# A fused streaming-encoder block: the weight sums of the short groups made in the output projection, part of the last operands split one block earlier

## The chip, the cores and the metric

The kernel runs on one core of a Trainium2 chip. The metric is the device time of one execution in microseconds (us). Three runs of the kernel before gave 2062.32, 2059.2 and 2062.35 us, a median of 2062.32 us.

In the text PE is the matrix engine, DVE the vector engine, ACT the scalar engine, POOL and SP the two engines that issue the DMA transfers. "hi" and "lo" are the two parts into which a 32-bit number is split for the matrix engine.

## The reference, cut to what matters

One layer works on 512 tokens of 2048 features: a mixer (convolution heads and gated linear attention), an output projection, and a feed-forward block of 8192 hidden features.

```python
y = concatenate([y_conv, y_gla], axis=-1)
x = x + y @ w_out                                   # output projection
h = rmsnorm(x, norm2_g)
x = x + square(relu(h @ w_ff1)) @ w_ff2             # feed-forward: FF1, FF2
return rmsnorm(x, norm_f_g)
```

All of it is in float32. The change touches how `w_ff2` is brought to the matrix engine for the last 1024 of the 8192 hidden features; what is computed stays the same.

## The kernel before, in words

**Products.** Every product of float32 operands is made of three passes on PE: hi times hi, hi times lo, lo times hi. For each tile of weights ACT makes hi (a cast) and DVE makes lo (raw minus hi). A product of two 2x2 arrangements of blocks is made in a scheme with seven products ("forms" 1 to 7) in place of eight. A form's weight operand is a quarter block (forms 1, 3, 2) or a sum of quarter blocks that DVE makes first (forms 5, 7, 6, 4), so DVE has four sums and seven lo tiles for each group of seven forms. `block_forms` (line 226) loads the four quarters on SP and makes sums and splits; `split_w` (line 212) is the split, whose ACT cast is on line 215 and DVE subtraction on line 216; `plus` is the sum on line 223.

**FF2.** The loop over `blk` (0 to 3) and `n` (0 to 3, the four quarters of the output features) runs two groups for each (blk, n). In blocks 0 to 2 a form has 24 matmuls in each group. In block 3 the first group is full and the second is *short*: half as many hidden features, so 12 matmuls for each form, while every form still needs its cast, its lo and, for four of them, its sum. In the second group `evict` (line 1014) takes the results out of PSUM: DVE makes t, x, v and four c tiles (line 1020), ACT scales each c in two pieces (line 1027), and POOL adds it to `c_keep` in DRAM with an accumulating DMA (line 1028).

**The last 512 hidden features** are not in any block. They come plain, in 16 groups `e_{i}{n}` of 12 matmuls (128x512 each) for four token tiles i and four output quarters n, in the order n = 0, 2, 1, 3. Their weight operands are w00, w01, w20, w21, w10, w11, w30, w31 (hi and lo of each), their activations e0 and e1. They are loaded and split after block 3's code: casts on line 1088, lo on line 1089. Each e group is added to x by DVE (line 1133), squared by ACT (line 1137) for the final norm.

**The output projection** comes earlier, in five chunks. In chunk 0 a unit has 24 matmuls of 128x512; DVE makes one lo for each unit and is idle for the rest of it. Its results are added to `xr`, the residual, whose 20 tiles POOL loads from `x`.

**What sets the order.** Each engine works through its own list in order. The lists are made by a scheduler, so that the place of an instruction there can differ from the code's. Raw weights come through one ring of four 512 KB slots (tag `raw`), hi and lo through rings of three, sums through a ring of two (tag `w`). A load is issued when the work that used its slot four loads before is done, and the loads stand in order on SP.

In names, `f_3114` is block 3, n = 1, group 1 (the short one), form 4, and `f_3201` is block 3, n = 2, group 0, form 1. `c_31` is a c tile of block 3, n = 1.

Of the kernel before, what the change touches and what calls it, by code (L numbers as in the profile page):

```python
# [8 lines left out]
F32 = mybir.dt.float32  # L9
# [5 lines left out]
P = 128  # L15
# [18 lines left out]
RAWS = 4  # L34
# [8 lines left out]
def hymba_kernel(  # L43
# [712 lines left out]
    for n, c in enumerate(chunks):  # L756
        for i in range(NT):
            nc.gpsimd.dma_start(xs[n][i], x[i * P : (i + 1) * P, c])
    ss2 = const_tile("ss2", [P, NT, 5])
# [53 lines left out]
    with tc.tile_pool(name="n2", bufs=1) as n2:  # L813
# [15 lines left out]

        for n in range(3):  # L830
            at = {2: (2 * n - 2,), 5: (2 * n - 1,)} if n else {}
            out_chunk(n, w_out, 8 * n, 8, 512, 2, pairs_at(at), w_ready if n == 0 else ())
# [166 lines left out]
    with tc.tile_pool(name="ff", bufs=1, reuse_waits="tile") as ff:  # L999
# [53 lines left out]

        for blk in range(4):
            for n in range(4):
                dst = {f: fbank(f"f2_{blk}{n}{f}") for f in ORDERS[1]}
                had = {}
                for grp in range(2):
                    m = 2 if (blk, grp) == (3, 1) else 4
                    src, i0 = (  # L1060
                        (w_ff2, 4 * (8 * blk + 2 * n + grp)) if blk < 3
                        else ((w_ff2, 4 * (24 + n)), (w_ff2_short, 4 * n))[grp]
                    )
                    forms = block_forms(src, i0, m * HALF, f"f2_{blk}{n}{grp}")
# [14 lines left out]
        slots = first + second[:7]  # L1079
        taken = [0]  # L1080

        def next_slot(name):
            taken[0] += 1
            return in_slot(slots[taken[0] - 1], name)

        def pair_split(src, name):
            hi, lo = next_slot(f"{name}h"), next_slot(f"{name}l")
            S.copy(hi, src)  # L1088
            V.tensor_tensor(out=lo, in0=src, in1=hi.bitcast(F32), op=ALU.subtract)
            return hi, lo  # L1090

        w2 = {}

        def last_weights(n):
            for j in range(2):
                raw = wp.tile([P, UNIT], F32, name=f"raw_e{n}{j}", tag="raw", bufs=RAWS)
                nc.sync.dma_start(raw[:, :1024], w_ff2_last[2 * n + j])
                hi, lo = pair_split(raw[:, :1024].rearrange("p (a b) -> p a b", a=4), f"w{n}{j}")
                for e in range(2):
                    w2[n, 2 * j + e] = [t[:, 2 * e : 2 * e + 2, :].rearrange("p a b -> p (a b)") for t in (hi, lo)]  # L1100

        load_x(3)
        order = (0, 2, 1, 3)
        last_weights(order[0])
# [19 lines left out]
        for i in range(NT):  # L1124
# [3 lines left out]
            for n in order:  # L1128
# [8 lines left out]
                S.activation(sq.rearrange("p a b -> p (a b)"), x3[n], AF.Square, accum_out=ss3[:, i, n : n + 1])  # L1137
# [18 lines left out]
def laid_out(inputs):  # L1156
# [29 lines left out]

    def feature_pairs(w):
# [25 lines left out]
        "w_ff2_short": quarters(ff2[7168:7680], 2).reshape(-1, P, 512),  # L1213
# [21 lines left out]
```

## Time and profile before

| | |
|---|---|
| median of three runs | 2062.32 us (2059.2 to 2062.35) |
| profiled execution, its own time | 2064.88 us |
| its span | 2063.2 us, so 1.68 us lie around it |
| PE busy | 2026.6 us, 98% of the span |
| DVE busy | 1594.4 us, 77% |
| ACT busy | 1018.4 us, 49% |
| POOL busy | 224.1 us, 11% |
| mean granted clock of PE | 0.996 |

A row of a timeline gives the start, the time taken, the engine, the line, the operation, its output and inputs, the shape and, in brackets, how long the engine was idle before it and what ended that. Matmuls overlap: the distance between two starts tells more than the time of one. A row of the view of waits gives total time, number of times and the longest.

### The profile page before, as it was taken

The page shows a single profiled execution, that of the slowest core. Times are in us where ns is not written, and L with a number is a line of the kernel's source. Part 1 is how long each engine was busy: PE and PEld are TensorE (multiplying, and loading weights), DVE is VectorE, ACT ScalarE, POOL GpSimd, SP SyncE. Part 2 cuts the span into 40 slices and gives each one's busy share as a digit, 9 for nine tenths or more (in the row PEclk, how much of TensorE's full clock was granted, in tenths as well). Part 3 has the DMA queues.
Part 4 walks back from the last instruction along what each step waited for, and adds up shares of the span by engine and source line. Part 5 has one row for each costly group of instructions (what it writes and reads, how often), then busy time and mean ns, then how long its engine had stood idle before and what let it go on. Part 6 is the DMA issues. An engine that isn't in the chain of part 4 may idle for free. (4 is left out here: it accounts for less than half of the span.)

```text
span 2063.2 us, 36979 instructions
## 1 busy us (share of the span) xinstructions
PE 2026.6 (98%) x15344; PEld 1945.0 (94%) x15344; DVE 1594.4 (77%) x1880; ACT 1018.4 (49%) x1366; POOL 224.1 (11%) x349
## 2 busy tenths in 40 slices
PE   8999999999999989999999999999999999999997
PEld 8999998888888889999999999999999999999995
DVE  8778775677734478888888888888789779788785
ACT  8434444433433345555555545555455445545453
POOL 1000001100020001000101001111011111111321
PEclk9999999999999999999999999999999999999999
DMA  8333335322253325545545545758477567657764
GB/s 283 128 124 133 132 135 180 123 87 72 82 197 111 110 82 176 174 147 183 168 147 177 164 163 165 220 178 274 126 226 217 148 193 232 150 164 236 169 186 119
DMA packets 112554, 334.57 MB, mean 162 GB/s; under 512 B 12213, under 2 KB 29157, under 8 KB 112384
## 3 DMA queue, kind: packets, MB, share of 16 engines
q1 hardware_dynamic: 60912, 210.92, 30.9%
q0 software_dynamic: 51472, 121.27, 21.2%
q8 instruction: 120, 1.97, 0.4%
q14 instruction: 50, 0.41, 0.1%
HBM read 263.20 MB, written 68.94 MB: 161 GB/s over the span
## 5 line engine op out<-in xcount | busy, mean ns | idle before, releaser
L1009 PE MATMUL f<-lo_f,ah 128*128 128x256 f32 x1568 | 442.3, 282 | 1.7 <-DVE lo_f L216 1.5
L1009 PE MATMUL f<-hi_f,ah 128*128 128x256 f32 x1568 | 440.3, 281 | 1.0 <-ACT hi_f L215 1.0
L1009 PE MATMUL f<-hi_f,al 128*128 128x256 f32 x1568 | 440.6, 281 | 0.0
L215 ACT CAST hi_f<-w_f 128x1024 fp32r<-128x1024 f32 (+1 forms) x256 | 261.5, 1023 | 337.4 <-PE f L1009 114.3
L216 DVE TENSOR_TENSOR lo_f<-w_f,hi_f 128x1024 fp32r<-128x1024 f32 (+1 forms) x256 | 304.8, 1191 | 150.0 <-ACT hi_f L215 148.9
L1009 PEld LDWEIGHTS f<-lo_f,ah 128*128 128x128 f32 x1568 | 295.5, 188 | 2.9 <-DVE lo_f L216 2.7
L1009 PEld LDWEIGHTS f<-hi_f,ah 128*128 128x128 f32 x1568 | 296.2, 189 | 1.4 <-ACT hi_f L215 1.4
L1009 PEld LDWEIGHTS f<-hi_f,al 128*128 128x128 f32 x1568 | 296.2, 189 | 0.0
L215 ACT CAST hi_f<-raw_f 128x1024 fp32r<-128x1024 f32 (+1 forms) x192 | 196.5, 1024 | 141.9 <-PE f1b L933 54.5
L216 DVE TENSOR_TENSOR lo_f<-raw_f,hi_f 128x1024 fp32r<-128x1024 f32 (+1 forms) x192 | 227.4, 1186 | 20.8 <-ACT hi_f L215 20.8
L223 DVE TENSOR_TENSOR w_f<-raw_f,raw_f 128x1024 f32<-128x1024 f32 (+1 forms) x128 | 152.4, 1190 | 14.4 <-DMA raw_f<-in_w_ff 9.1
L223 DVE TENSOR_TENSOR w_f<-w_f,raw_f 128x1024 f32<-128x1024 f32 (+1 forms) x128 | 152.3, 1190 | 3.6 <-DMA raw_f<-in_w_ff 0.3
L933 PE MATMUL f1c<-Sh,hi_f 128*128 128x256 f32 x512 | 144.5, 282 | 0.9 <-ACT q L957 0.9
L933 PE MATMUL f1a<-Sh,hi_f 128*128 128x256 f32 x512 | 145.3, 284 | 0.0
L933 PE MATMUL f1a<-Sh,lo_f 128*128 128x256 f32 x512 | 145.2, 284 | 0.0
L933 PE MATMUL f1a<-Sl,hi_f 128*128 128x256 f32 x512 | 145.1, 283 | 0.0
L933 PE MATMUL f1c<-Sh,lo_f 128*128 128x256 f32 x512 | 144.5, 282 | 0.2 <-DVE lo_f L216 0.2
L933 PE MATMUL f1c<-Sl,hi_f 128*128 128x256 f32 x512 | 144.3, 282 | 0.0
L78 PE MATMUL tm_op<-hi_op,yh 128*128 128x512 f32 (+1 forms) x304 | 106.3, 350 | 0.0
L79 PE MATMUL tm_op<-lo_op,yh 128*128 128x512 f32 (+1 forms) x304 | 105.4, 347 | 0.0
L80 PE MATMUL tm_op<-hi_op,yl 128*128 128x512 f32 (+1 forms) x304 | 105.1, 346 | 0.0
L1028 POOL DMA_DIRECT2D c_keep<-c x64 | 56.4, 900 | 385.9 <-ACT c L1027 292.6
(521 smaller groups left out, 5564.7 us busy)
## 6 DMA issues: line engine op xcount, KB each, us to landing
raw_f<-in_w_ff SPq DMA_DIRECT2D x240, 512.0 KB, 3.4
st<-a_keep POOLq DMA_DIRECT2D x33, 512.0 KB, 5.2
c_keep<-c POOLq DMA_DIRECT2D x64, 256.0 KB, 4.9
a_keep<-y POOLq DMA_DIRECT2D x14, 896.0 KB, 4.8
raw_op<-in_w_out SPq DMA_DIRECT2D x22, 512.0 KB, 3.3
raw_v<-in_w_v SPq DMA_DIRECT2D x16, 512.0 KB, 3.5
raw_og<-in_w_pairs SPq DMA_DIRECT2D x16, 512.0 KB, 3.3
raw_cc<-in_w_feat SPq DMA_DIRECT2D x16, 512.0 KB, 3.7
```

Source lines behind the costliest of these rows:

```text
L78: T.matmul(dst, l[0], r[0], start=start, stop=False)
L79: T.matmul(dst, l[0], r[1], start=False, stop=False)
L80: T.matmul(dst, l[1], r[0], start=False, stop=stop)
L215: S.copy(hi[:, :n], src)
L216: V.tensor_tensor(out=lo[:, :n], in0=src, in1=hi[:, :n].bitcast(F32), op=ALU.subtract)
L223: V.tensor_tensor(out=w, in0=in0, in1=in1, op=ALU.add)
L933: T.matmul(dst[:, :HALF], l[:, c], r, start=start and p == m == 0, stop=p == 7 and m == 2, skip_group_check=True,)
L1009: T.matmul(d, l[:, k, t], r[:, c], start=grp == k == i == e == 0, stop=grp == 1 and k == m - 1 and e == 2, skip_group_check=True,)
L1028: nc.gpsimd.dma_start(c_keep[n][q], t, accum_op=ALU.add)
```

## The change

Three things are done.

1. **The sums of the four short groups** (16 DVE additions of 128x512) are made during chunk 0 of the output projection, after its units 1, 3, 5 and 7. `sum_short(n)` loads the four quarters in two loads of 512 KB through the raw ring, makes the four sums in two tiles of the `w` ring, and POOL stores these two tiles (512 KB each) in DRAM scratch `short_sums`. In block 3 a short group then loads two tiles of quarters and two of ready sums (`short_forms`: three loads of 512 KB and one of 256 KB, where before there were four of 256 KB) and makes no sum. The host lays `w_ff2_short` out anew so that forms 1 and 3 lie in one tile.
2. **Part of the last operands is split earlier**: e0 and e1 in the first group of (3, 1), w00 in the first group of (3, 2). They and w01 go to tiles of the `stage` pool and a new ring `early`. The activations e0 and e1 come through the raw ring.
3. **ACT's squares** of token tile 0 are ordered behind the last weight cast (`issue_after`), and `gft` is loaded later.

```diff
@@ -756,6 +758,25 @@
+
+    short_sums = [[tc.dram_tile([P, 1024], F32, name=f"short{n}{m}") for m in range(2)] for n in range(4)]
+
+    def sum_short(n):
+        raws = []
+        for m in range(2):
+            raw = wp.tile([P, UNIT], F32, name=f"raw_s{n}{m}", tag="raw", bufs=RAWS)
+            nc.sync.dma_start(raw[:, :1024], w_ff2_short[2 * n + m])
+            raws.append((raw[:, :512], raw[:, 512:1024]))
+        (b12, b21), (b11, b22) = raws
+        w56, w47 = (sums[-1].tile([P, 1024], F32, name=f"w_s{n}{m}", tag="w", bufs=2) for m in range(2))
+        for out_, i0, i1 in (
+            (w56[:, :512], b11, b12), (w56[:, 512:], w56[:, :512], b21),
+            (w47[:, :512], w56[:, 512:], b22), (w47[:, 512:], b11, b21),
+        ):
+            V.tensor_tensor(out=out_, in0=i0, in1=i1, op=ALU.add)
+        for m, w in enumerate((w56, w47)):
+            nc.gpsimd.dma_start(short_sums[n][m], w)
+
...
@@ -827,9 +848,13 @@
+        def shorts(j):
+            if j % 2:
+                sum_short(j // 2)
+
         for n in range(3):
             at = {2: (2 * n - 2,), 5: (2 * n - 1,)} if n else {}
-            out_chunk(n, w_out, 8 * n, 8, 512, 2, pairs_at(at), w_ready if n == 0 else ())
+            out_chunk(n, w_out, 8 * n, 8, 512, 2, pairs_at(at) if n else shorts, w_ready if n == 0 else ())
...
@@ -1051,22 +1076,77 @@
 
+        def short_forms(n):
+            v = {}
+            for m, (src, c, fs) in enumerate((
+                (w_ff2_short[2 * n], 0, (1, 3)), (short_sums[n][0], 0, (5, 6)),
+                (short_sums[n][1], 0, (4, 7)), (w_ff2_short[2 * n + 1], 512, (2,)),
+            )):
+                raw = wp.tile([P, UNIT], F32, name=f"raw_f{n}{m}", tag="raw", bufs=RAWS)
+                nc.sync.dma_start(raw[:, c:1024], src[:, c:])
+                for i, f in enumerate(fs):
+                    v[f] = raw[:, c + 512 * i : c + 512 * (i + 1)]
+            return lambda f: split_w(v[f], 512, f"f2_3{n}1{f}")
+
+
+        early = [(stage, "st", 4)] * 4 + [(ff, "early", 2)] * 2
+        slots = [slot + (1,) for slot in first + second[:7]]
+        taken = [0]
+
+        def next_slot(name):
+            if early:
+                pool, tag, bufs = early.pop(0)
+            else:
+                pool, tag, bufs = slots[taken[0]]
+                taken[0] += 1
+            return pool.tile([P, 4, HALF], F32R, name=name, tag=tag, bufs=bufs)
+
+        def pair_split(src, name):
+            hi, lo = next_slot(f"{name}h"), next_slot(f"{name}l")
+            last_cast[0] = S.copy(hi, src)
+            V.tensor_tensor(out=lo, in0=src, in1=hi.bitcast(F32), op=ALU.subtract)
+            return hi, lo
+
+        w2 = {}
+
+        def last_weights(n, j):
+            raw = wp.tile([P, UNIT], F32, name=f"raw_e{n}{j}", tag="raw", bufs=RAWS)
+            nc.sync.dma_start(raw[:, :1024], w_ff2_last[2 * n + j])
+            hi, lo = pair_split(raw[:, :1024].rearrange("p (a b) -> p a b", a=4), f"w{n}{j}")
+            for e in range(2):
+                w2[n, 2 * j + e] = [t[:, 2 * e : 2 * e + 2, :].rearrange("p a b -> p (a b)") for t in (hi, lo)]
+
+        order = (0, 2, 1, 3)
+        a = []
+
+        def last_acts(g):
+            raw = wp.tile([P, UNIT], F32, name=f"raw_a{g}", tag="raw", bufs=RAWS)[:, :1024]
+            raw = raw.rearrange("p (a b) -> p a b", a=4)
+            nc.sync.dma_start(raw, a_last[g])
+            hl = pair_split(raw, f"e{g}")
+            for e in range(2):
+                a.append([[t[:, (1, 0, 2, 3)[2 * e + row], :] for t in hl] for row in range(2)])
+
+
+        early_at = {
+            (1, 2): lambda: last_acts(0), (1, 5): lambda: last_acts(1), (2, 3): lambda: last_weights(order[0], 0),
+        }
+
         for blk in range(4):
             for n in range(4):
                 dst = {f: fbank(f"f2_{blk}{n}{f}") for f in ORDERS[1]}
                 had = {}
                 for grp in range(2):
                     m = 2 if (blk, grp) == (3, 1) else 4
-                    src, i0 = (
-                        (w_ff2, 4 * (8 * blk + 2 * n + grp)) if blk < 3
-                        else ((w_ff2, 4 * (24 + n)), (w_ff2_short, 4 * n))[grp]
-                    )
-                    forms = block_forms(src, i0, m * HALF, f"f2_{blk}{n}{grp}")
+                    src, i0 = w_ff2, 4 * (8 * blk + 2 * n + grp if blk < 3 else 24 + n)
+                    forms = short_forms(n) if m == 2 else block_forms(src, i0, 1024, f"f2_{blk}{n}{grp}")
                     for f in ORDERS[grp]:
                         product2(blk, grp, f, m, dst[f], *forms(f))
                         if grp == 1:
                             evict(blk, n, f, dst, had)
                         on_agenda(8 * blk + 2 * n + grp, ORDERS[grp].index(f))
+                        if (blk, grp) == (3, 0):
+                            early_at.get((n, ORDERS[0].index(f)), lambda: None)()
...
@@ -1076,42 +1156,10 @@
-        slots = first + second[:7]
-        taken = [0]
-
-        def next_slot(name):
-            taken[0] += 1
-            return in_slot(slots[taken[0] - 1], name)
-
...
-        def last_weights(n):
-            for j in range(2):
-                raw = wp.tile([P, UNIT], F32, name=f"raw_e{n}{j}", tag="raw", bufs=RAWS)
...
         load_x(3)
-        order = (0, 2, 1, 3)
-        last_weights(order[0])
-        a = []
-        for g in range(2):
-            raw = stage.tile([P, 4, HALF], F32, name=f"st_e{g}", tag="st", bufs=4)
-            nc.sync.dma_start(raw, a_last[g])
-            hl = pair_split(raw, f"e{g}")
-            for e in range(2):
-                a.append([[t[:, (1, 0, 2, 3)[2 * e + row], :] for t in hl] for row in range(2)])
-        for n in order[1:]:
-            last_weights(n)
-        gft = [stage.tile([P, 4, HALF], F32, name=f"gft{c}", tag="st", bufs=4) for c in range(2)]
+        for n, j in [(n, j) for n in order for j in range(2)][1:]:
+            last_weights(n, j)
+        gft = [next_slot(f"gft{c}").bitcast(F32) for c in range(2)]
...
@@ -1134,7 +1182,8 @@
                 sq = ff.tile([P, 2, HALF], F32, name=f"sq3_{n}{i}", tag="c", bufs=4)
-                S.activation(sq.rearrange("p a b -> p (a b)"), x3[n], AF.Square, accum_out=ss3[:, i, n : n + 1])
+                with tc.issue_after(last_cast[0].ins) if i == 0 else nullcontext():
+                    S.activation(sq.rearrange("p a b -> p (a b)"), x3[n], AF.Square, accum_out=ss3[:, i, n : n + 1])
...
@@ -1183,6 +1232,10 @@
                               f2[6].reshape(-1, P, 1024)])
+
+
+    short = quarters(ff2[7168:7680], 2)[:, [0, 2, 1, 3]].reshape(4, 2, 2, P, 512)
+    short = np.ascontiguousarray(short.transpose(0, 1, 3, 2, 4)).reshape(-1, P, 1024)
 
```

The first place is the turn from the short group of (3, 1) to the first group of (3, 2) on DVE. Before:

```order
L216 TENSOR_TENSOR lo_f_3112_21334<-raw_f_3113_21227,hi_f_3112_21333 128x512
L223 TENSOR_TENSOR w_f_3205_21475<-raw_f_3201_21385,raw_f_3200_21383 128x1024
L1020 TENSOR_TENSOR c_31_21303<-f_313_20999,x_21285 128x512
L1020 TENSOR_TENSOR v_21326<-f_317_21000,t_21267 128x512
L1020 TENSOR_TENSOR c_31_21328<-f_317_21000,x_21285 128x512
L1020 TENSOR_TENSOR c_31_21349<-f_312_21001,q_21245 128x512
L216 TENSOR_TENSOR lo_f_3114_21356<-w_f_3116_21249,hi_f_3114_21355 128x512
L216 TENSOR_TENSOR lo_f_3201_21392<-raw_f_3200_21383,hi_f_3201_21391 128x1024
L223 TENSOR_TENSOR w_f_3207_21505<-raw_f_3201_21385,raw_f_3202_21387 128x1024
L1020 TENSOR_TENSOR c_31_21371<-f_314_21002,v_21326 128x512
```

and now:

```order
L1045 TENSOR_TENSOR c_31_21360<-f_313_21048,x_21342 128x512
L218 TENSOR_TENSOR lo_f_3114_21410<-raw_f_21286,hi_f_3114_21409 128x512
L225 TENSOR_TENSOR w_f_3205_21529<-raw_f_3201_21439,raw_f_3200_21437 128x1024
L1045 TENSOR_TENSOR v_21381<-f_317_21049,t_21324 128x512
L1045 TENSOR_TENSOR c_31_21383<-f_317_21049,x_21342 128x512
L1045 TENSOR_TENSOR c_31_21404<-f_312_21050,q_21306 128x512
L1045 TENSOR_TENSOR c_31_21425<-f_314_21051,v_21381 128x512
L218 TENSOR_TENSOR lo_f_3201_21446<-raw_f_3200_21437,hi_f_3201_21445 128x1024
L218 TENSOR_TENSOR lo_f_3203_21474<-raw_f_3202_21441,hi_f_3203_21473 128x1024
```

The lo of form 4 (`lo_f_3114`) now stands ahead of the next block's sum and the three evictions; the lo of the next block's form 1 (`lo_f_3201`), which stood ahead of the last eviction (`c_31` from `f_314`), now stands behind it.

The second place is ACT after the last short group. Before:

```order
L1027 ACTIVATE c_33_22131<-c_33_22131,r_5739 128x256 x2
L1088 CAST w11h<-raw_e_22186 128x1024
L1088 CAST w30h<-raw_e_22192 128x1024
L1137 ACTIVATE sq_00_22223,ss_22208<-x_00_20830 128x512
L1137 ACTIVATE sq_20_22240,ss_22208<-x_01_20831 128x512
L1088 CAST w31h<-raw_e_22198 128x1024
```

and now:

```order
L1052 ACTIVATE c_33_22177<-c_33_22177,r_5747 128x256 x2
L1106 CAST w11h<-raw_e_22214 128x1024
L1106 CAST w30h<-raw_e_22220 128x1024
L1106 CAST w31h<-raw_e_22226 128x1024
L1186 ACTIVATE sq_00_22251,ss_22236<-x_00_20886 128x512
```

Two squares stood between the casts of w30 and w31; now they stand behind both.

The third place is DVE at the end of chunk 0 of the output projection, as it is now (`w_s` are the sums of the fourth short group; before, none of the four `w_s` rows is there):

```order
L76 TENSOR_TENSOR lo_op_0_6057<-raw_op_0_6055,hi_op_0_6056 128x1024
L776 TENSOR_TENSOR w_s_6023<-raw_s_6021,raw_s_6019 128x512
L776 TENSOR_TENSOR w_s_6024<-raw_s_6021,raw_s_6019 128x512
L776 TENSOR_TENSOR w_s_6023<-w_s_6023,raw_s_6019 128x512
L776 TENSOR_TENSOR w_s_6024<-w_s_6023,raw_s_6021 128x512
L76 TENSOR_TENSOR lo_op_1_6087<-raw_op_1_6085,hi_op_1_6086 128x1024
L839 TENSOR_TENSOR xr_5698<-tm_op_5751,xr_5698 128x512
```

The four sums stand between the lo tiles of units 0 and 1 of chunk 1 (`lo_op_0`, `lo_op_1`) and ahead of the additions of chunk 0's results (`xr`, line 839). They write the two tiles from which POOL stores the third group's sums, and these two stores stand behind POOL's 20 loads of `xr`:

```order
L760 DMA xr_5715<-in_x 128x256
L760 DMA xr_5716<-in_x 128x256
L760 DMA xr_5717<-in_x 128x256
L778 DMA short_5742<-w_s_5951 128x1024
L778 DMA short_5743<-w_s_5952 128x1024
L778 DMA short_5744<-w_s_6023 128x1024
```

Before, POOL's list went from the last load of `xr` to the first `c_keep` store.

More of the change, by code (lines that the diff above doesn't have):

```diff
@@ L1 @@
-from contextlib import ExitStack
+from contextlib import ExitStack, nullcontext
 import concourse.bass as bass
@@ L60, in const_tile @@
         return const.tile(shape, dt, name=name, tag=name)
+    last_cast = [None]
     def unit(src, n, name, pieces=1, before=None):
@@ L1076, in hymba_kernel @@
                             load_x(n - 1)
-        slots = first + second[:7]
-        taken = [0]
-        def next_slot(name):
-            taken[0] += 1
-            return in_slot(slots[taken[0] - 1], name)
[L1086 to L1092, printed above, removed]
-        def last_weights(n):
-            for j in range(2):
-                raw = wp.tile([P, UNIT], F32, name=f"raw_e{n}{j}", tag="raw", bufs=RAWS)
-                nc.sync.dma_start(raw[:, :1024], w_ff2_last[2 * n + j])
-                hi, lo = pair_split(raw[:, :1024].rearrange("p (a b) -> p a b", a=4), f"w{n}{j}")
-                for e in range(2):
-                    w2[n, 2 * j + e] = [t[:, 2 * e : 2 * e + 2, :].rearrange("p a b -> p (a b)") for t in (hi, lo)]
-        load_x(3)
-        order = (0, 2, 1, 3)
-        last_weights(order[0])
-        a = []
-        for g in range(2):
-            raw = stage.tile([P, 4, HALF], F32, name=f"st_e{g}", tag="st", bufs=4)
-            nc.sync.dma_start(raw, a_last[g])
-            hl = pair_split(raw, f"e{g}")
-            for e in range(2):
-                a.append([[t[:, (1, 0, 2, 3)[2 * e + row], :] for t in hl] for row in range(2)])
-        for n in order[1:]:
-            last_weights(n)
-        gft = [stage.tile([P, 4, HALF], F32, name=f"gft{c}", tag="st", bufs=4) for c in range(2)]
+        load_x(3)
+        for n, j in [(n, j) for n in order for j in range(2)][1:]:
+            last_weights(n, j)
+        gft = [next_slot(f"gft{c}").bitcast(F32) for c in range(2)]
         for c in range(2):
@@ L1212, in laid_out @@
         "w_ff2": f2_full,
-        "w_ff2_short": quarters(ff2[7168:7680], 2).reshape(-1, P, 512),
+        "w_ff2_short": short,
         "w_ff2_last": units(ff2[7680:], 2, 512),
```

## The prediction

> **What bounds the kernel now.** I read the page first, then the waits of PE, then the timelines of the places the change touches.
>
> ```profile
> span 2063.2 us, 36979 instructions
> PE 2026.6 (98%) x15344; PEld 1945.0 (94%) x15344; DVE 1594.4 (77%) x1880; ACT 1018.4 (49%) x1366; POOL 224.1 (11%) x349
> ```
>
> PE is busy for 98% of the span: the kernel is bound by its matmuls, and the change removes none. It can only gain where PE waits, so the view of PE's waits lists what can be had:
>
> ```profile
> PE f L1009 <- DVE lo_f L216: 5.5, 7, 1.2
> PE htr L779 <- DVE xr L818: 4.5, 4, 3.1
> PE e L78 <- ACT w31h L1088: 2.6, 1, 2.6
> PE e L79 <- DVE w30l L1089: 0.8, 1, 0.8
> ```
>
> Row 2 is at 750 to 756 us, which the change leaves alone. Rows 3 and 4 lie after the last short group, and most of row 1 at the ends of the four. Here is one such end, the turn from (3, 1) to (3, 2), first on PE, then on DVE:
>
> ```profile
> 1930.90 0.28 PE L1009 MATMUL f<-hi_f,a 128*128 128x256 f32 x1
> 1931.02 0.28 PE L1009 MATMUL f<-lo_f,a 128*128 128x256 f32 x1
> 1939.51 0.28 PE L1009 MATMUL f<-hi_f,ah 128*128 128x256 f32 x1
> 1941.02 0.39 PE L1009 MATMUL f<-lo_f,a 128*128 128x256 f32 x1 [1.24 <-DVE lo_f L216]
> 1942.42 0.28 PE L1009 MATMUL f<-lo_f,ah 128*128 128x256 f32 x1
> ```
> ```profile
> 1932.54 0.69 DVE L223 TENSOR_TENSOR w_f<-raw_f,raw_f 128x512 f32<-128x512 f32 x1
> 1936.06 0.68 DVE L216 TENSOR_TENSOR lo_f<-raw_f,hi_f 128x512 fp32r<-128x512 f32 x1
> 1936.75 1.23 DVE L223 TENSOR_TENSOR w_f<-raw_f,raw_f 128x1024 f32<-128x1024 f32 x1
> 1939.69 0.68 DVE L1020 TENSOR_TENSOR c<-f,q 128x512 f32<-128x512 f32 x1
> 1940.29 0.68 DVE L216 TENSOR_TENSOR lo_f<-w_f,hi_f 128x512 fp32r<-128x512 f32 x1
> 1940.88 1.22 DVE L216 TENSOR_TENSOR lo_f<-raw_f,hi_f 128x1024 fp32r<-128x1024 f32 x1
> ```
>
> The short group starts at 1930.90 (call it T), and matmuls follow each other by (1939.51 - 1930.90) / 73 = 0.118 us, so a form of 12 lasts 1.42 us and seven last 9.94. PE waits 1.24 us for the lo of form 4, made at 1940.29, because DVE had a sum for the next block, v and three c ahead of it. The next block's form 1 goes on at 1942.42, T+11.52. Its lo (1940.88) was ready at 1942.10, so it costs no second wait. The turns before and after show the same wait, three in all.
>
> After the fourth short group PE and ACT read:
>
> ```profile
> 1993.36 0.28 PE L1009 MATMUL f<-hi_f,a 128*128 128x256 f32 x1
> 2013.53 0.50 PE L79 MATMUL e<-w30l,e0h 128*128 128x512 f32 x1 [0.76 <-DVE w30l L1089]
> 2017.57 0.80 PE L78 MATMUL e<-w31h,e1h 128*128 128x512 f32 x1 [2.61 <-ACT w31h L1088]
> 2018.16 0.63 PE L78 MATMUL e<-w00h,e0h 128*128 128x512 f32 x1
> 2020.72 0.41 PE L78 MATMUL e<-w31h,e1h 128*128 128x512 f32 x1
> 2021.43 0.40 PE L79 MATMUL e<-w00l,e0h 128*128 128x512 f32 x1
> 2022.36 0.39 PE L80 MATMUL e<-w01h,e1l 128*128 128x512 f32 x1
> ```
> ```profile
> 2012.13 0.62 ACT L1137 ACTIVATE sq<-x 128x512 f32<-128x512 f32 x1
> 2015.86 0.63 ACT L1137 ACTIVATE sq<-x 128x512 f32<-128x512 f32 x1 [3.01 <-DMA c_keep<-c]
> 2016.48 1.03 ACT L1088 CAST w31h<-raw_e 128x1024 fp32r<-128x1024 f32 x1
> ```
>
> ACT's square at 2015.86 waits 3.01 us for a transfer, and the cast of w31 stands behind it in ACT's list; PE waits 2.61 us for that cast. After the wait the e matmuls follow each other at (2020.72 - 2018.16) / 6 = 0.43 us, before falling back to (2022.36 - 2021.43) / 4 = 0.2325. From 1993.36 to 2021.43 PE needs 84 x 0.118 + 52 x 0.2325 = 22.0 us (52 = the 48 e matmuls of token tile 0 and four of tile 1 that slipped in) and takes 28.07. So 6.0 us are lost at this end.
>
> **The change, part by part.**
>
> *The end, -5.0.* With the squares behind all weight casts, and w00, e0 and e1 split earlier, what is late next is the load of w31: the ring has four slots, and its load waits for DVE to finish w21's lo. In the new DVE list from lo_12 (T+5.8 if lo_12 ends as in the turn above, 1936.74) stand five narrow operations at 0.60 before w21's lo, and three wide ones at 1.13 with it: T+12.2. The loads of these weights land as follows:
>
> ```profile
> DMA to landing us min/median/max: 3.2/4.3/6.7
> ```
>
> So it lands at T+16.5 by the median, cast and lo take 1.03 and 1.22 (T+18.8), and PE comes to w31 at T + 9.94 + 42 x 0.2325 = T+19.7. It just fits. With the longest landing it is T+21.2 and PE waits 1.5. I leave 1.0 us of waits there and at w11 and w30: 6.0 - 1.0 = 5.0 gained, between 3.5 and 5.8. The 0.43 pace goes with the wait that brings it.
>
> *The three turns, +1.9.* The sums leave DVE, and lo_14 now stands before the next block's sum: from 1936.66 DVE does c (0.60), lo_14 (0.60), the sum (1.13), v, c, c (1.80) and is free at 1940.8. Form 4 no longer waits and ends at T+9.94 = 1940.84. But the lo of the next form 1 now stands behind the eviction of form 4, which cannot start before PE has finished form 4. So: start of the eviction 1941.0, 0.60 later the lo, 1.22 for it: 1942.8, and PE goes on at 1942.9 in place of 1942.42. PE has only two hi matmuls (0.24) to fill that, and waits 1.8 us where it waited 1.24. That is 0.5 us more for each turn. If the next block's raws land late (they now wait for slots that lo_15, lo_13 and lo_12 free), the sum and all behind it slip by up to 0.4:
>
> ```profile
> raw_f<-in_w_ff SPq DMA_DIRECT2D x4, 512.0 KB, 3.8
> raw_f<-in_w_ff_short SPq DMA_DIRECT2D x2, 256.0 KB, 7.3
> ```
>
> (issues from 1926 to 1946 us; the 7.3 are loads that met the c_keep accumulations). The second raw, issued at T+3.4 after lo_13, lands at T+7.2 by 3.8, which is the time at which the sum would start. So 0.5 to 0.9 for each turn, and I take 0.63, 1.9 for three. The wait is moved, not removed.
>
> *Early splits, +0.6.* The two casts and lo tiles of e0 and e1 go into the first group of (3, 1), whose form 7 has its cast behind theirs on ACT. Before, these activations landed as this row says:
>
> ```profile
> DMA to landing us min/median/max: 4.9/6.1/7.3
> ```
>
> The load of e1 is issued after DVE's sum for form 7, some 4 us into the group. With 4.9 it lands at 9 and two casts (2 x 1.03) reach form 7's start, 4 forms x 2.83 = 11.3, just in time; with 7.3 form 7 waits some 1.9. I take 0.6, between 0 and 1.9. The split of w00 stands between forms of a full group, where DVE has time: it was busy 24.95 of 32 us in this stretch.
>
> ```profile
> 1930.00:1962.00 32.00, 30.77 (x261) 30.56 (x260) 24.95 (x30) 15.40 (x23) 7.97 (x12) 1.00 0.66 165
> ```
>
> *The projection, +0.3.* The sixteen sums (as the one at 1932.54) cost 16 x 0.69 = 11 us of DVE, and DVE is idle there:
>
> ```profile
> 553.10 0.69 DVE L673 TENSOR_TENSOR up<-fm_ch,cc 128x512 f32<-128x512 f32 x1 [1.22 <-PE fm_ch L80]
> 604.66 1.23 DVE L74 TENSOR_TENSOR lo_op<-raw_op,hi_op 128x1024 fp32r<-128x1024 f32 x1 [4.29 <-ACT hi_op L73]
> 605.80 1.28 DVE L818 TENSOR_TENSOR xr<-tm_op,xr 128x512 f32<-128x512 f32 x2
> 594.46 0.54 POOL L758 DMA_DIRECT2D xr<-in_x  x1 [0.62 <-DMA xr<-in_x]
> ```
>
> A unit leaves 4.29 us, four sums take 2.8. Only the fourth set is tight. It writes the tiles that the third set's stores read, and those stand on POOL behind the last `xr` load (594.46, and some 3 us later now, since the sums delay the norm tiles that these loads wait for). At 5 us a store lands near 602 to 603; then the sums run to 605.5, the lo of unit 1 to 606.7, and the first `xr` addition comes near 607 instead of 605.80. PE wants that bank back when chunk 0 ends, near 609.0. If the stores are 3 us later the wait is about 2. I take 0.3, between 0 and 2. The 8 loads and 8 stores of 512 KB themselves lie in a stretch whose loads are issued one for each 5.5 us unit.
>
> *Sum:* -5.0 + 1.9 + 0.6 + 0.3 = -2.2 us. The profiled execution took 2064.88 us (span 2063.2, 1.68 around it), so 2062.7 by its clock. The median is 2.56 lower, and this kernel has also run 2059.2; I take the sum from the median: **2060.1 us**. Two measurements of this kernel can be told apart from about 0.2%, 4.1 us, so this is a small gain that may not be seen.
>
> **The rivals.**
>
> *A. The turns lose their wait altogether.* For it: DVE has 2.8 us less to do in each short group (four sums of 0.69), and lo_14 does come in time. Against it: the eviction of form 4 stands ahead of the next lo and needs PE's last matmul. Then the turns give 3 x 1.24 = -3.7 in place of +1.9: 2060.1 - 5.6 = 2054.5 us, clearly faster. Chance 0.08.
>
> *B. The clock falls at the turns.* [...] Two waits of this trace were followed by slow matmuls, the one of 2.61 us above and this one:
>
> ```profile
> 755.67 0.69 PE L779 MATMUL htr<-ident,xr 128*128 128x128 f32 x2 [3.15 <-DVE xr L818]
> 756.58 0.42 PE L933 MATMUL f1a<-Sh,lo_f 128*128 128x256 f32 x1
> 757.00:758.00 1.00, 1.00 (x6) 1.00 (x6) 1.00 (x3) 0.52 (x1) 0.00 (x0) 0.50 0.37 131
> 2018.00:2019.00 1.00, 1.00 (x3) 0.73 (x3) 1.00 (x2) 0.00 (x0) 0.57 (x2) 0.50 0.88 234
> ```
>
> The granted clock (the third figure from the end) is 0.50 after both. After 1.24 us it stayed at 1.00 (the window from 1930). A wait of 1.8 to 2.2 us lies between. After 2.61 us the slow pace cost (2020.72 - 2017.57) - 7 x 0.2325 = 1.5 us. Three turns of 1.5 to 2.4 with a wait at the longer end (+0.8) give +5.3 to +8: 2060.1 + 6.5 = 2066.6 us, slower than before. Chance 0.22.
>
> By the Trainium skill, "TensorE: Matmul & The Clock Gate", section "HAM oscillation — how this bites in real kernels", PE must stand idle for more than about 3.4 us before its clock is halved; by that rule B could not happen at all and the sum would stay as it is. The wait of 2.61 us with a clock of 0.50 behind it speaks against the rule as a sharp limit, so it does not remove B here.
>
> *C. The early loads cost more*: the splits of e0 and e1 at 1.9 and the fourth set at 2: +3.0 over the sum, 2063.1 us, no change to be seen, and slower with a turn at its upper end. Chance 0.12.
>
> *D. The end gains little*, because the later weights land at 6.7 us each among the accumulations and the wait for w31 comes back: +3.0, 2063.1 us. Chance 0.10.
>
> **How the numbers follow.** The forecast has 0.48, with a range of its own from 2057 to 2062.5: of this 0.19 lies over 4.1 us below the median, 0.27 within, 0.02 above. A adds 0.08 to faster; B 0.10 to the same and 0.12 to slower; C 0.05 and 0.07; D 0.08 and 0.02. Faster 0.27, the same 0.50, slower 0.23. The range leaves out the far half of A and of B: 2055.0 to 2067.5.
>
> **What would show it.** Right: PE's waits at the three turns for lo of form 1 of the next block, 1.7 to 2.2 us, and none for form 4; no wait for w31h over 1.6 us, and 21.5 to 23 us from the fourth short group's start to the end of token tile 0's e groups; the squares behind w31's cast. B shows in a granted clock of 0.5 behind a turn. C shows as a wait of form 7 of the first group of (3, 1) for hi_f, or of PE near 609 us for `xr`. Wrong: no wait at the turns (A), or a wait of over 2 us at w31 (D).

## The result and the profile after

The changed kernel takes 2075.74 us (median of six runs, 2069.13 to 2078.33); the kernel before takes 2061.83 us beside it (six runs). The ratio is 1.0064, with a 95% interval from 1.0049 to 1.0078: some 13 us slower, where 2 us faster had been forecast. The profiled execution took 2078.33 us. Its page:

```profile
span 2076.6 us, 36998 instructions
PE 2032.2 (98%) x15344; PEld 1947.1 (94%) x15344; DVE 1594.9 (77%) x1880; ACT 1017.7 (49%) x1366; POOL 228.3 (11%) x357
```

DVE does the same work as before (1594.9 against 1594.4 us). In both traces PE's longest wait is one for `uh` (6.9 us before, 6.7 now). Next comes a row that before has not, for `tm_op`; these rows of the view matter here:

```profile
PE tm_op L80 <- DVE xr L839: 5.3, 1, 5.3
PE f L1034 <- ACT hi_f L217: 4.5, 6, 1.3
PE htr L800 <- DVE xr L839: 4.3, 4, 2.8
PE f L1034 <- DVE lo_f L218: 4.2, 7, 1.2
PE eab_ps L262 <- DVE eab_d L265: 3.4, 1, 3.4
PE e L81 <- DVE w31l L1107: 0.8, 1, 0.8
PE e L81 <- DVE w30l L1107: 0.6, 1, 0.6
PE e L80 <- ACT w31h L1106: 0.5, 1, 0.5
```

Both traces have 15344 matmuls, in nearly the same order, so the start of the n-th in the one can be set against that of the n-th in the other. The growth of this difference over a stretch says where time went (times of the kernel before):

| stretch | after minus before, us |
|---|---|
| start to 562: before chunk 0, code that the change hardly touches | +1.9 |
| 562 to 614: chunk 0 of the output projection and what follows it | +9.6 |
| 614 to 1898: rest of the projection, FF1, blocks 0 to 2 and the first group of (3, 0) | +0.7 |
| 1898 to 1991: the three turns | +3.7 |
| 1991 to 2021: last short group and token tile 0's e groups | -2.3 |

**Chunk 0.** PE ends chunk 0 near 612.3 and cannot start chunk 1 before DVE has emptied the bank. PE and two windows of its clock:

```profile
617.67 0.77 PE L80 MATMUL tm_op<-hi_op,yh 128*128 128x512 f32 x1 [5.34 <-DVE xr L839]
618.23 0.63 PE L81 MATMUL tm_op<-lo_op,yh 128*128 128x512 f32 x1
617.00:618.00 1.00, 0.33 (x1) 0.36 (x2) 1.00 (x2) 0.40 (x1) 0.18 (x1) 0.50 0.91 246
618.00:624.00 6.00, 6.00 (x15) 4.66 (x15) 2.54 (x4) 3.11 (x9) 3.56 (x7) 0.51 1.00 393
```

The wait is 5.34 us, and 6 us at a granted clock of 0.51 follow it (the third figure from the end), which cost some 3 us more. The other 1.3 us are lost near 571 us, where PE waits 0.84 us for a DVE result: DVE had stood idle 2.67 us before a sum of the first set (556.47). DVE, then ACT and POOL at the end of chunk 0:

```profile
586.36 0.69 DVE L106 TENSOR_TENSOR yl<-y,yh 128x512 fp32r<-128x512 f32 x1 [0.69 <-ACT yh L105]
610.04 1.23 DVE L76 TENSOR_TENSOR lo_op<-raw_op,hi_op 128x1024 fp32r<-128x1024 f32 x1 [6.08 <-ACT hi_op L75]
612.58 0.69 DVE L776 TENSOR_TENSOR w_s<-raw_s,raw_s 128x512 f32<-128x512 f32 x1 [1.32 <-DMA short<-w_s]
615.70 1.22 DVE L76 TENSOR_TENSOR lo_op<-raw_op,hi_op 128x1024 fp32r<-128x1024 f32 x1
616.83 2.48 DVE L839 TENSOR_TENSOR xr<-tm_op,xr 128x512 f32<-128x512 f32 x4
```
```profile
608.96 1.05 ACT L75 CAST hi_op<-raw_op 128x1024 fp32r<-128x1024 f32 x1 [6.26 <-DMA raw_op<-in_w_out]
587.70 1.61 POOL L760 DMA_DIRECT2D xr<-in_x  x3 [3.60 <-DVE yl L106]
605.59 0.54 POOL L760 DMA_DIRECT2D xr<-in_x  x1 [0.79 <-DMA xr<-in_x]
606.69 0.54 POOL L778 DMA_DIRECT2D short<-w_s  x1 [0.56 <-DMA xr<-in_x]
```

And before, the last yl and the first loads of xr:

```profile
577.98 0.68 DVE L104 TENSOR_TENSOR yl<-y,yh 128x512 fp32r<-128x512 f32 x1
579.30 3.71 POOL L758 DMA_DIRECT2D xr<-in_x  x7 [141.45 <-DVE yl L104]
```

The chain reads backwards: the xr additions (616.83) stand behind the fourth set's sums (612.58), which wait for the third set's stores (issued 606.69), which stand on POOL behind the last xr load (605.59), and these loads began at 587.70 in place of 579.30, because the last yl tile (586.36 in place of 577.98) came later. Of these 8.4 us, 1.9 are the shift that the whole trace has from its first 562 us. For the other 6.5, DVE's rows show eight sums of the first two sets ahead of yl (0.60 us each, from 556.47 to 582.59), and DVE idle for 2.67, 1.97 and 0.32 us before three of them, the last two for a load and a store.

A second strand runs beside this one. The raw weights of unit 0 of chunk 1 came late too, so that their cast waited 6.26 us (608.96, against 598.06 before) and their lo, which stands ahead of the fourth set, was made at 610.04. Behind it the stores held DVE for 1.32 us and then 0.49 us more.

**A turn.** The turn from (3, 1) to (3, 2), PE and then DVE:

```profile
1954.97 0.38 PE L1034 MATMUL f<-hi_f,ah 128*128 128x256 f32 x1 [1.14 <-ACT hi_f L217]
1956.00 0.39 PE L1034 MATMUL f<-lo_f,ah 128*128 128x256 f32 x1 [0.65 <-DVE lo_f L218]
```
```profile
1951.19 1.22 DVE L225 TENSOR_TENSOR w_f<-raw_f,raw_f 128x1024 f32<-128x1024 f32 x1 [0.35 <-DMA raw_f<-in_w_ff]
1954.13 0.68 DVE L1045 TENSOR_TENSOR c<-f,v 128x512 f32<-128x512 f32 x1
1954.73 2.35 DVE L218 TENSOR_TENSOR lo_f<-raw_f,hi_f 128x1024 fp32r<-128x1024 f32 x2
```

PE no longer waits for form 4; it waits 1.14 us for hi of the next block's form 3 (one matmul of which PE has taken forward) and 0.65 us more for lo of form 1: 1.79 in all.

**The end.** The squares stand behind the casts, and w31's cast now waits for its load. The last row is the view of all eight loads of the last weights:

```profile
2027.35 1.05 ACT L1106 CAST w30h<-raw_e 128x1024 fp32r<-128x1024 f32 x1 [1.19 <-DMA raw_e<-in_w_ff_last]
2030.54 1.05 ACT L1106 CAST w31h<-raw_e 128x1024 fp32r<-128x1024 f32 x1 [2.15 <-DMA raw_e<-in_w_ff_last]
DMA to landing us min/median/max: 3.3/5.6/6.8
```

### The profile page after: what moved, and what is told of

Read it like the earlier page. It is cut to its first block, busy times and chain, and to the rows that moved or that the text cites. A ratio compares the mean times of both kernels' runs of the same rounds, so it can differ in the third digit from the quotient of the medians.

```text
span 2076.6 us, 36998 instructions
## 1 busy us (share of the span) xinstructions
PE 2032.2 (98%) x15344; PEld 1947.1 (94%) x15344; DVE 1594.9 (77%) x1880; ACT 1017.7 (49%) x1366; POOL 228.3 (11%) x357
## 3 DMA queue, kind: packets, MB, share of 16 engines
q8 instruction: 120, 1.97, 0.4%
## 5 line engine op out<-in xcount | busy, mean ns | idle before, releaser
L217 ACT CAST hi_f<-w_f 128x1024 fp32r<-128x1024 f32 x240 | 251.7, 1050 | 318.8 <-PE f L1034 94.4
L218 DVE TENSOR_TENSOR lo_f<-w_f,hi_f 128x1024 fp32r<-128x1024 f32 x240 | 293.7, 1225 | 144.2 <-ACT hi_f L217 143.1
L217 ACT CAST hi_f<-raw_f 128x1024 fp32r<-128x1024 f32 (+1 forms) x208 | 206.4, 992 | 164.5 <-PE f1b L958 54.5
L218 DVE TENSOR_TENSOR lo_f<-raw_f,hi_f 128x1024 fp32r<-128x1024 f32 (+1 forms) x208 | 238.6, 1148 | 40.8 <-ACT hi_f L217 40.7
L225 DVE TENSOR_TENSOR w_f<-raw_f,raw_f 128x1024 f32<-128x1024 f32 x120 | 146.9, 1224 | 13.5 <-DMA raw_f<-in_w_ff 10.2
L225 DVE TENSOR_TENSOR w_f<-w_f,raw_f 128x1024 f32<-128x1024 f32 x120 | 146.8, 1224 | 3.3 <-DMA raw_f<-in_w_ff 0.2
L958 PEld LDWEIGHTS f1c<-Sh,hi_f 128*128 128x128 f32 x512 | 96.8, 189 | 1.1 <-ACT q L982 1.1
```

Of the source, the lines that this page charges most:

```text
L217: S.copy(hi[:, :n], src)
L218: V.tensor_tensor(out=lo[:, :n], in0=src, in1=hi[:, :n].bitcast(F32), op=ALU.subtract)
L225: V.tensor_tensor(out=w, in0=in0, in1=in1, op=ALU.add)
L958: T.matmul(dst[:, :HALF], l[:, c], r, start=start and p == m == 0, stop=p == 7 and m == 2, skip_group_check=True,)
```

## The experiments

There were eleven experiments. This table gives, for each, the median, its ratio to the kernel before on the same chip with the 95% interval, and from its trace the difference to the trace of before over the same stretches as above. The first stretch, which the edits hardly touch, moves between -2.7 and +3.8 us from execution to execution, so a single time says little here and the stretches say more. Each stretch is read from one trace.

| | median us | ratio | start-562 | 562-614 | 614-1898 | turns | end |
|---|---|---|---|---|---|---|---|
| the change | 2075.74 | 1.0064 (1.0049 to 1.0078) | +1.9 | +9.6 | +0.7 | +3.7 | -2.3 |
| e1 sums in chunks 1, 2 | 2066.16 | 1.0020 (1.0005 to 1.0035) | -2.1 | 0.0 | +0.6 | +3.2 | -1.7 |
| e2 early splits, squares | 2065.49 | 1.0026 (1.0008 to 1.0044) | +3.8 | 0.0 | +1.2 | +3.9 | -2.6 |
| e3 sums only | 2073.22 | 1.0061 (1.0046 to 1.0076) | -1.1 | +7.9 | -1.2 | +5.1 | -0.4 |
| e4 fourth set later | 2075.50 | 1.0076 (1.0053 to 1.0099) | +1.2 | +10.7 | +0.3 | +5.3 | -0.3 |
| e5 e1 + late evictions | 2061.72 | 0.9996 (0.9983 to 1.0009) | -1.4 | -0.1 | -0.2 | -1.4 | -3.0 |
| e6 late evictions only | 2060.89 | 0.9989 (0.9977 to 1.0001) | +3.2 | 0.0 | +0.4 | -4.1 | +1.3 |
| e7 late evictions, squares | 2057.38 | 0.9969 (0.9958 to 0.9981) | -2.7 | 0.0 | -1.9 | -4.2 | -2.9 |
| e8 squares only | 2060.43 | 0.9991 (0.9979 to 1.0003) | -2.3 | -0.1 | -0.6 | -0.1 | -2.7 |
| e9 e7 + sums in chunks 1, 2 | 2058.51 | 0.9989 (0.9978 to 1.0000) | -2.6 | -0.1 | +0.4 | -1.8 | -1.6 |
| e10 fourth set in chunk 2 | 2067.31 | 1.0037 (1.0026 to 1.0048) | -0.2 | +0.9 | -0.9 | +4.3 | -1.5 |
| e11 e7 again | 2055.33 | 0.9977 (0.9966 to 0.9989) | +1.1 | -0.1 | -0.1 | -4.1 | +0.3 |

e1 to e4 ran on one chip (before 2060.38 us), e5 to e8 on one (2062.53), e9 to e11 on one (2061.08). Kernels of different chips are compared by their ratios. The edits are against the changed kernel where nothing else is said; `...` marks lines left out.

### e1: the sums in chunks 1 and 2

```diff
-            if j % 2:
-                sum_short(j // 2)
...
+                if n in (1, 2) and j in (0, 4):
+                    sum_short(2 * (n - 1) + j // 4)
```

> The four sets of sums are made in chunks 1 and 2 of the output projection (after units 0 and 4 of each) and no longer in chunk 0; all else is as in the change. Theory P (the loss is the end of chunk 0: the sums hold up the norm tiles, so the xr loads, so the third set's stores, so the fourth set's sums, and the xr additions stand behind those; PE waited 5.3 us there and then ran 6.8 us at half clock): no wait for xr over 1 us near 610 us, and 2062 to 2065 us, some 10 to 13 us under the change. Rival Q (the loss is the sixteen sums, eight loads and eight stores wherever they stand in the projection, or lies in block 3): 2070 us or more.

Chunk 0 lost nothing (0.0), and the ratio fell from 1.0064 to 1.0020 (2066.16 us). So the whole loss of that stretch is where the sums stood, not that they were made in the projection: theory P. The median lies 1.2 us above the expected span.

### e2: the early splits and the squares, without moving sums

```diff
...
-                    forms = short_forms(n) if m == 2 else block_forms(src, i0, 1024, f"f2_{blk}{n}{grp}")
...
+                    forms = block_forms(src, i0, m * HALF, f"f2_{blk}{n}{grp}")
```

> Only the second and third part of the change: e0, e1 and w00 split early and the squares behind the last weight cast; the short groups load quarters and make their sums as before. P: no wait for xr near 609 us, the turns wait 1.2 us as before, and after the last short group 3.5 to 4.5 us are lost where before lost 6.0, so 1 to 3 us under the kernel before: 2059 to 2061. Rival (the early splits cost in block 3 what they give at the end): 2062 or more.

This missed: it is slower than the kernel before. PE waits inside the first groups, where before it did not; here in that of (3, 1), at its forms 7 and 4:

```profile
1928.01 0.38 PE L1012 MATMUL f<-hi_f,ah 128*128 128x256 f32 x1 [0.44 <-ACT hi_f L217]
1929.27 0.39 PE L1012 MATMUL f<-lo_f,ah 128*128 128x256 f32 x1 [0.88 <-DVE lo_f L218]
1935.69 0.39 PE L1012 MATMUL f<-lo_f,ah 128*128 128x256 f32 x1 [0.49 <-DVE lo_f L218]
```

With w00's wait (0.58 us at 1968.27) the three turns lose 3.9 us, more than the 2.6 us that the end gives back. The rival holds: where DVE still has the short groups' sums, the early splits take from block 3 what they give. The end itself lost something too: ACT's cast of w20 now stood ahead of a cast of the last short group and waited 3.55 us for its load, and PE waited 1.62 us for the cast behind it:

```profile
2011.04 1.04 ACT L1071 CAST w20h<-raw_e 128x1024 fp32r<-128x1024 f32 x1 [3.55 <-DMA raw_e<-in_w_ff_last]
2012.65 0.39 PE L1012 MATMUL f<-hi_f,a 128*128 128x256 f32 x1 [1.62 <-ACT hi_f L217]
```

### e3: the sums in chunk 0 alone

```diff
-        early = [(stage, "st", 4)] * 4 + [(ff, "early", 2)] * 2
...
-                        if (blk, grp) == (3, 0):
-                            early_at.get((n, ORDERS[0].index(f)), lambda: None)()
...
-                with tc.issue_after(last_cast[0].ins) if i == 0 else nullcontext():
```

> Only the first part of the change: the sums in chunk 0 and the short groups from scratch; the last operands are loaded and split as before. P: the wait for xr of 4 to 6 us with the half clock behind it is there, the turns wait 1.8 us, and the end loses 5 to 6 us as before: 2072 to 2080, at or above the change. Rival (the loss comes from the early splits): 2064 or less.

The wait for xr is 4.4 us with half clock behind it, the turns lose 5.1 us (half clock behind two of them), and the end gains only 0.4. As expected by P: the first part of the change alone has a loss as large as the whole change (ratio 1.0061 against 1.0064).

### e4: the fourth set written later

```diff
-                sum_short(j // 2)
...
+                if n == 0 and j in (1, 3, 5):
+                    sum_short(j // 2)
+                if n == 1 and j == 1:
+                    sum_short(3)
```

> As the change, but the fourth set of sums is made after unit 1 of chunk 1, so that only three sets are in chunk 0. If the fourth set's sums ahead of the xr additions are the last link of the chain (P): the wait for xr falls from 5.3 us to under 2 us, no half clock behind it, 2065 to 2069. If the xr loads themselves, made late by the first three sets, are already too late for chunk 0's end: a wait of 3 us or more stays and the time is over 2070.

The expected fall did not come (wait 6.7 us), but it says nothing against the chain: in DVE's list the four sums had kept their place ahead of the xr additions, waiting 7.71 us for the same stores. Here the raw weights of unit 0 of chunk 1 came before the fourth set's (its lo was made by 605.41), so the wait for the stores is enough by itself, without the second strand.

```profile
613.12 0.69 DVE L776 TENSOR_TENSOR w_s<-raw_s,raw_s 128x512 f32<-128x512 f32 x1 [7.71 <-DMA short<-w_s]
617.33 2.48 DVE L839 TENSOR_TENSOR xr<-tm_op,xr 128x512 f32<-128x512 f32 x4
```

### e10: the fourth set really behind the xr additions

Against e4:

```diff
-                if n == 1 and j == 1:
+                if n == 2 and j == 0:
```

> As the change, with the fourth set of sums written in chunk 2, so that in DVE's list its four sums really stand behind the xr additions of chunk 0 (in e4 they had kept their place). If the fourth set's sums, waiting for the third set's stores, are what holds the xr additions: the wait for xr falls from 5.3 us to under 1.5 us, no half clock behind it, and the stretch from 562 to 614 us takes 1 to 3 us more than before instead of 9.6: 2063 to 2069. If the xr loads themselves come too late: a wait of 3 us or more stays.

Here DVE's list did change, and the first xr addition comes at once:

```profile
605.32 1.23 DVE L76 TENSOR_TENSOR lo_op<-raw_op,hi_op 128x1024 fp32r<-128x1024 f32 x1 [1.88 <-ACT hi_op L75]
606.47 1.28 DVE L839 TENSOR_TENSOR xr<-tm_op,xr 128x512 f32<-128x512 f32 x2
585.07 1.61 POOL L760 DMA_DIRECT2D xr<-in_x  x3 [3.60 <-DMA raw_s<-in_w_ff_short]
601.65 0.54 POOL L760 DMA_DIRECT2D xr<-in_x  x1 [0.79 <-DMA xr<-in_x]
```

No wait for xr is left, the stretch costs 0.9 us in place of 9.6, and the ratio falls from 1.0064 to 1.0037, some 5.6 us (2067.31 us). The first and the last xr load (585.07 and 601.65) are still 6 and 7 us later than before (6.5 and 9.2 in the change); they were not too late. The fourth set in chunk 0, its sums behind two stores and its loads, makes nearly all of the loss there.

### e5: e1 with late evictions

Against e1:

```diff
-                        if grp == 1:
+                        if grp == 1 and m == 2 and n < 3 and f in (7, 2, 4):
+                            held.append((blk, n, f, dst, had))
+                        elif grp == 1:
                             evict(blk, n, f, dst, had)
+                        if grp == 0:
+                            while held:
+                                evict(*held.pop(0))
```

> As e1 (sums in chunks 1 and 2, early splits, squares last), and the evictions of forms 7, 2 and 4 of the first three short groups are written behind form 1 of the next group, so that on DVE the lo of that form 1 stands ahead of three c tiles. Theory T (PE's wait at a turn is DVE's list: lo of form 1 behind sum, v and three c; the half clock behind a turn follows from the length of that wait): the waits at the three turns fall from about 1.8 us to 0.2 to 0.8, no half clock behind any, so 3 x 1.2 + some 2 = 5 to 6 us under e1: about 2060. Rival (the wait is for the raw loads that now wait for later slots, and hi of form 3): waits of 1.1 us or more stay, gain under 2 us.

In DVE's list the lo of the next form 1 now stands behind the sum and v, ahead of the three c. PE's waits at the three turns:

```profile
1908.38 0.38 PE L1038 MATMUL f<-lo_f,ah 128*128 128x256 f32 x1 [0.16 <-DVE lo_f L218]
1939.87 0.38 PE L1038 MATMUL f<-lo_f,ah 128*128 128x256 f32 x1 [0.31 <-DVE lo_f L218]
1973.27 0.39 PE L1038 MATMUL f<-hi_f,ah 128*128 128x256 f32 x1 [0.18 <-ACT hi_f L217]
```

0.16 to 0.31 us in place of 1.4 to 1.6 in e1, and no half clock; the ratio falls from 1.0020 to 0.9996, some 4.9 us, a little less than the 5 to 6 expected. Theory T holds. With every part of the change in it and its two faults mended, the kernel stands where the kernel before stands (interval 0.9983 to 1.0009).

### e6, e8, e7 and e11: the lists put in order, and nothing moved

e6 has the late evictions of e5 on the kernel before, e8 only the squares behind the last cast, e7 both, and e11 is e7 again. The edit of e8, against the kernel before:

```diff
-            S.copy(hi, src)
+            last_cast[0] = S.copy(hi, src)
...
-                S.activation(sq.rearrange("p a b -> p (a b)"), x3[n], AF.Square, accum_out=ss3[:, i, n : n + 1])
+                with tc.issue_after(last_cast[0].ins) if i == 0 else nullcontext():
+                    S.activation(sq.rearrange("p a b -> p (a b)"), x3[n], AF.Square, accum_out=ss3[:, i, n : n + 1])
```

> The kernel before with the late evictions alone: no sums moved, nothing split early. By T's durations lo of form 4 is done at T+8.2 (needed at 8.6) and lo of form 1 at T+10.0 (needed at 10.1), that of form 3 at 12.9 (needed at 12.8): the 1.2 us waits at the turns go without moving any sum, 3.5 us under the kernel before, 2057 where it has 2060.4. Rival (DVE has too much to do in a short group, so the wait only moves to form 3 or later): within 1 us of the kernel before.

> The kernel before with the squares of token tile 0 behind the last weight cast alone. If ACT's order made the wait for w31: wait under 1.5 us, no half clock, 2 to 3.5 us under the kernel before. If the load of w31 is late itself (issued after w21's lo): the wait stays over 2 us, no change.

> The kernel before with the late evictions and with the squares of token tile 0 behind the last weight cast; no sums moved, nothing split early. T: 3.5 us from the turns, and at the end the wait of 2.61 us for w31 falls below 1.5 us and the half clock behind it goes (1.5 us): 5 to 7 us under the kernel before, 2053.5 to 2055.5. Rival (w31's load is late itself): the end gives under 1 us.

> e7 once more, on the chip of e9: 0.997 of the kernel before, 5 us under it, if the first comparison holds.

In e6 the turns lose their wait and give 4.1 us, with all sums still on DVE. The median is 1.6 us lower, with an interval that touches 1: by time alone e6 is not settled. In its trace the old wait for w31, 2.13 us this time, is followed by half clock:

```profile
2017.82 0.79 PE L78 MATMUL e<-w31h,e1h 128*128 128x512 f32 x1 [2.13 <-ACT w31h L1094]
2018.00:2020.00 2.00, 2.00 (x5) 1.61 (x6) 1.69 (x2) 0.23 (x1) 1.55 (x4) 0.50 0.81 248
```

In e8 the wait for w31's cast falls from 2.61 to 0.20 us, and the end gives 2.7; its median is 2.1 us lower, with an interval that touches 1, so that here too only the trace shows the gain:

```profile
2010.60 0.50 PE L79 MATMUL e<-w30l,e0h 128*128 128x512 f32 x1 [0.76 <-DVE w30l L1089]
2012.22 0.50 PE L78 MATMUL e<-w31h,e1h 128*128 128x512 f32 x1 [0.20 <-ACT w31h L1088]
2013.48 0.50 PE L79 MATMUL e<-w31l,e1h 128*128 128x512 f32 x1 [0.76 <-DVE w31l L1089]
```

e7 has both, -4.2 and -2.9, and all that PE waits for in block 3 and at the end of its trace is

```profile
1987.77 0.38 PE L1009 MATMUL f<-hi_f,a 128*128 128x256 f32 x1 [0.17 <-ACT hi_f L215]
1989.12 0.38 PE L1009 MATMUL f<-lo_f,a 128*128 128x256 f32 x1 [0.96 <-DVE lo_f L216]
2004.72 0.50 PE L78 MATMUL e<-w30h,e0h 128*128 128x512 f32 x1 [0.21 <-ACT w30h L1094]
2005.98 0.50 PE L79 MATMUL e<-w30l,e0h 128*128 128x512 f32 x1 [0.76 <-DVE w30l L1095]
```

It takes 2057.38 and, run again, 2055.33 us: 0.9969 (0.9958 to 0.9981) and 0.9977 (0.9966 to 0.9989). Both intervals lie under 1, so it is faster than the kernel before and the changed one, by 0.2 to 0.3% of the former. The 5 to 7 us under the kernel before that were expected of e7 came (5.2 us by the medians), though its own time lies 2 us above the expected span. e11's profiled execution was its slowest (2063.2 us), with half clock from 2013.63 us on behind waits of 0.76 and 1.02 us close together; so its end reads +0.3.

### e9: e7 with the sums moved to chunks 1 and 2

Against e7:

```diff
+                if n in (1, 2) and j in (0, 4):
+                    sum_short(2 * (n - 1) + j // 4)
...
-                    forms = block_forms(src, i0, m * HALF, f"f2_{blk}{n}{grp}")
+                    forms = short_forms(n) if m == 2 else block_forms(src, i0, 1024, f"f2_{blk}{n}{grp}")
```

> As e7 (late evictions, squares last), with the short groups' sums made in chunks 1 and 2 of the projection as in e1; nothing split early. It asks what moving the sums is worth once DVE's list at the turns is in order. If DVE's work still bounds the short groups: the waits that e7 has left in the fourth short group (0.17 and 0.96 us) go, 1 to 2 us under e7. If the turns were a matter of order alone: within 1.5 us of e7, or up to 2 us over it where the next group's raw loads, which now wait for later slots, come late (waits for hi of 0.2 to 1 us at a turn).

Its median is 3.2 us above that of e11 on the same chip, more than the 2 us allowed for. The waits of the fourth short group went, but the turns kept 0.4 to 0.5 us each for lo of form 1 and gave 1.8 us where e7 and e11 gave 4.1 to 4.2. At the end it gave 1.6 us, less than e7's 2.9. With DVE's list in order, moving the sums gains nothing; by these runs it costs.

## Why the prediction was wrong, point by point

**The projection (+0.3 forecast, +9.6 measured) is the step that failed.** The chain was named (the fourth set behind the third's stores, these behind the xr loads), and its sizes were wrong. "Some 3 us later" for the xr loads was 6.5 for the first of them (587.70 against 579.30, less the 1.9 us by which the trace of the change runs late from its first stretch) and 9.2 for the last (605.59 against 594.46, less the same). The sums' own time was counted, and not that sums of the first two sets would wait in DVE's list for loads and stores of their own, with the yl tiles behind them. The last xr load then came at 605.59 in place of 597, and the first store landed at 612.6, 5.9 us after its issue, and not at 602 to 603; the 5 us taken for a store came from no row. That the raw weights of chunk 1 would come late behind the fourth set's loads (unit 0's cast at 608.96; at 601.14 in e10, where these loads are gone from there) was not in the sum at all. The row that should have warned is the one quoted for the idle DVE: an engine that idles 4.29 us of each unit still blocks whatever stands behind a waiting instruction. And the bound of 2 us left out the clock: a wait of 5.3 us brought 6 us of half speed.

**The turns (+1.9 forecast, +3.7 measured).** The waits came out nearly as worked out: 1.42, 1.79 and 1.78 us where 1.7 to 2.2 had been written, and none for form 4. Without the clock the turns cost 2.0 us, so the place in the sum was right in size, though hi of form 3 took a share of the wait, and in the one turn read here the eviction of form 4 did not have to wait for PE: DVE was not free before 1954.13. What failed was the chance of 0.22 given to rival B as a case of its own: half clock followed the third turn and added some 1.7 us. It is no rival, it is a part of the price.

**The early splits (+0.6 forecast).** In the change PE waits nowhere in the first group of (3, 1) or (3, 2). But e2, with DVE fuller, shows the wait at form 7 that the step described, 1.3 us (0.44 for hi and 0.88 for lo).

**The end (-5.0 forecast, -2.3 measured).** The stretch took 25.8 us, where 21.5 to 23 had been named as the sign of being right: 3.8 us are still lost, where 1.0 had been left. PE's waits there are 0.35 us at w11, 0.58 at w30, and 0.49 and 0.77 at w31. The wait for w31's cast did fall as forecast, but w31's load was sized too short: it was issued at 2023.70 (T+14.4 with T = 2009.30, where T+12.2 was worked out; before it was T+14.2) and took 6.8 us (before 6.7), where the median of before, 4.3, had been put in the sum. The median of these loads rose to 5.6 us; why is not shown, for before, too, seven of them came within 11.3 us, now within 12.8. The gain can be had by the squares' order alone: e8, which has nothing else, gives 2.7 us there. What the early splits add at the end stays open: e5 with them gives 3.0 where e9 without them gives 1.6, but e2 with them gives no more than e8.

**Rivals.** A (the turns lose their wait) needed another edit, that of e5 and e6. Of C (early loads cost more) the half about the fourth set came, at 9.6 us where 2 was its bound; the half about e0 and e1 did not. B came in one turn of three. D came by its size, 2.7 us less at the end than forecast, though not by its sign, a wait of over 2 us at w31.

## What to carry to other kernels

An idle engine is room only for work that never waits: before work is put into an engine's idle time, look at what each new instruction waits for and at what stands behind it in the same list, two links further than the first. When an engine seems too slow at a hand-over, first put what the next stage needs ahead of what nobody waits for: late evictions and squares in the right order gave some 5 us, with no work moved, where moving the work lost 13. And price a wait of PE with the slow clock that may follow it, some 1.7 us for each 3.41 us at half speed. In these traces it followed when 1.5 us or more of idle time fell into one window of the clock, as the next section shows.

## What the runs showed of the hardware that was not expected

The clock falls after shorter waits than the 2.61 us of the trace before. In five runs (the change, e1, e3, e4, e10) the waits at the fifteen turns add up to 1.40 to 2.10 us each. Behind seven of them the granted clock was 0.50 for 3.4 us: waits of 1.51, 1.52, 1.55, 1.76, 1.78, 1.84 and 1.93 us. Behind eight it stayed at 1.00: 1.40, 1.41, 1.42, 1.56, 1.58, 1.67, 1.79 and 2.10 us. At the nine turns of before, e2 and e8, with 1.14 to 1.24 us, it never fell. So between 1.5 and 2.1 us the length of a wait does not decide. Behind the third turn of the change, and behind its first:

```profile
1990.00:1992.00 2.00, 2.00 (x11) 2.00 (x11) 1.51 (x2) 0.49 (x1) 1.98 (x4) 0.50 0.70 201
1925.00:1928.00 3.00, 3.00 (x28) 3.00 (x27) 2.33 (x3) 1.68 (x2) 1.65 (x3) 1.00 0.78 232
```

In the clock records of these traces every stretch of half clock inside the span lasts 3.41, 6.83 or 10.24 us, one, two or three times 3.41. The Trainium skill, "TensorE: Matmul & The Clock Gate", section "Part 1: The HAM clock gate (the "warmup" mystery)", says that the activity window is 3413 ns long and runs free of the program. The lengths agree with it. The traces also show where these windows lie: in each of the thirteen, all changes of the granted clock stand whole numbers of 3.4133 us apart (before, 754.39 and 2017.32 us: 370 times).

What decides is how much of PE's idle time, the gaps before its matmuls, falls into one window. Of all windows at full clock between the first and the last matmul of the thirteen traces, the 32 with 1.67 us or more of idle time were all followed by half clock, and none with 1.42 us or less was; of six between, with 1.51 to 1.62 us, four were. At half clock, 0.66 us or more in a window kept it there, and 0.48 us or less let it rise. The 2.10 us at the first turn of e10 fell as 1.18 and 0.92 us into two windows, and the clock stayed at 1.00. That a whole window must be idle, as the same page of the Trainium skill has it, does not agree: 1.5 us of waiting was enough.

The first 562 us, nearly the same code in all kernels, differ by up to 6.5 us between traces; the wait of PE for eab_d at 336 us alone (3.4 us in the change, 0.9 in e1, 1.2 before) with half clock behind it or not makes some 4 us of it. Why it differs stays open.
